# Low-rank products of RWKV-7 as split float32r products, shared scratch, and a changed order of the first receptance, in a fused decoder block on one core

## The chip, the cores and the metric

The kernel runs on one core of one Trainium2 chip. The metric is the device time of one execution in microseconds (us), the median of several runs. One execution is also taken by the hardware profiler; its span, from the first to the last instruction, is what the views of the profile divide up. PE is TensorE's matmul side, PEld its weight loads, DVE VectorE, ACT ScalarE, POOL GpSimd, SP the engine that issues the weight loads from memory.

## The reference, cut to what matters

The whole is one decoder layer for 512 tokens of width 1024: a norm, a combined projection, an attention mixer (NSA), an RWKV-7 mixer, a merge, an output projection, and a convolutional MLP. The change lies in the vectors that the RWKV-7 mixer prepares before its recurrence:

```python
def rwkv7_mixer(p_in, mu, w0, w2, a0, a2, g2, k_k, k_a, r_k, ln_g, ln_b):
    shifted = jnp.pad(p_in, ((0, 0), (1, 0), (0, 0)))[:, :-1]
    xl = p_in + (shifted - p_in) * mu
    r, k, v, xw, xa, xg = jnp.split(xl, RWKV_SPLITS, axis=-1)
    w = -jax.nn.softplus(-(w0 + jnp.tanh(xw) @ w2)) - 0.5
    decay = jnp.exp(-jnp.exp(w))
    a = jax.nn.sigmoid(a0 + xa @ a2)
    g = jax.nn.sigmoid(xg) @ g2
    ...
    kk = k * k_k
    kk = kk / jnp.maximum(jnp.sqrt(jnp.sum(kk * kk, axis=-1, keepdims=True)), 1e-12)
    k = k * (1.0 + (a - 1.0) * k_a)
    ...
```

The two low-rank products are tanh(xw) @ w2 (decay) and xa @ a2 (learning rate): 512 tokens, depth 64 each, 512 channels out.

## The kernel before, in words

**Layout.** Activations stand with channels on the 128 partitions and the 512 tokens along the free dimension, so a "dense" product of one weight tile (1024 deep, 128 channels) fills one PSUM bank of 128x512. The normalised input is kept as two float32r parts, hh and hl; each weight tile is loaded by SP into `raw` (three buffers), copied by ACT to its float32r high part `whi` and subtracted by DVE (some by POOL) to the low part `wlo` (two buffers each). A dense product (`dense_fm`, recorded at L120) is 24 passes of 512 columns: eight of whi by hh and eight of whi by hl in turn, then eight of wlo by hh. `wnext` issues the next load and the next split whenever a tile is taken.

**Who sets the order.** Engines run their own instructions in a fixed order and wait on semaphores. In parts marked `manual_schedule` that order is as written. Elsewhere, and so in all of the part around the change, a planner sets it when the program is built: it follows estimated times, and among instructions that it takes to be ready it prefers the one written earlier. Tiles with one tag share one buffer; a new tile of a tag waits until all users of the old one are done.

**The RWKV preparation (about 20 to 124 us).** p0 is the dense product that yields xw (rows 0 to 63) and xa (rows 64 to 127). `shift_mix` mixes each token with the one before it (ACT at L123, DVE at L135); tanh is taken of xw's half. `sg` comes from a second dense product. wa holds w2 on partitions 0 to 63 and a2 on 64 to 127; POOL issues its two loads (L435, L436), and g2's (L437). POOL then issues the loads of later parameters into prb and cr. Then, for each of four head pairs p:

- `front(p)`: the dense key product pk, then the two low-rank products: zw (`wa[0:64]` by `xw[0:64]`, bank ps_a) and za (`wa[64:128]` by `xw[64:128]`, bank ps_b), both in float32. From zw come cl (tanh), its running sum cum within chunks of 64 tokens, and the exponentials ep and pi; from za comes aa.
- `norms(p)`: kk, the squared scaled keys (ACT), then the sum over each head as a product with the block matrix `ones` in float32 (ps_a<-kk,kc), then rn by DVE's maximum and ACT's Ln and Exp.
- `receptance(p)`, `values_of(p)`: dense products r and v, mixed into rx and vx.
- `vectors(p)` (DVE): AR from rx and ep, kk times rn, bh (keys by pi), tv (rx by r_k by kx); tv's sum over heads is another product with `ones` (ps_a<-tv,kc), which gives BO.
- `values_tok(p)` (L540) and `gram(p)` (L571 and on): transposes of vx and bh, and products of bh and AR, masked into AB.

The order written is `front(0)`, `norms(0)`, `receptance(0)`, `values_of(0)`, `late_params()` (transposes of prb and cr, L478 to L483), and then the loop over p, with `front(p + 1)` and `norms(p + 1)` ahead of `vectors(p)`. The weight tiles come in the order key, receptance, value of each pair.

**After it.** DVE inverts 64 small triangular matrices (transposes at L623, 31 steps, transposes at L728 and L733) beside dense products; PE reads the inverse in `below` (32x32 products). Then come the recurrence, with g2 used in its group norm, attention, the merge and the MLP.

Of the kernel before, what the change touches and what calls it, by code (L numbers as in the profile page):

```python
# [10 lines left out]
F32 = mybir.dt.float32  # L11
F32R = mybir.dt.float32r
I32 = mybir.dt.int32
AF = mybir.ActivationFunctionType
ALU = mybir.AluOpType
# [4 lines left out]
S = 512  # L20
# [27 lines left out]
NROWS = _n  # L48
NR0 = ROWS["ffn_norm_g"][0]
# [31 lines left out]
def hybrid_block(ctx: ExitStack, tc: tile.TileContext, A: dict, out: bass.AP):  # L81
    nc = tc.nc
# [16 lines left out]
    def pool(name, side="left"):  # L99
        cm = tc.tile_pool(name=name, bufs=1, side=side)  # L100
        return cm, cm.__enter__()

    def close(cm):
        cm.__exit__(None, None, None)
# [8 lines left out]
    def pa():  # L113
        return bank("a", 2)

    def pb():
        return bank("b", 2)

    def mm(o, l, r, start, stop):
        te.matmul(o, lhsT=l, rhs=r, start=start, stop=stop)  # L120

    def act(o, i, f=AF.Copy, **kw):
        sc.activation(o, i, f, **kw)  # L123

    def tt(o, a, b, op):
        v.tensor_tensor(o, a, b, op=op)  # L126

    def ts(o, a, s1, s2, op0=ALU.mult, op1=ALU.add):
        if s2 is None:
            v.tensor_scalar(o, a, s1, None, op0=op0)  # L130
        else:
            v.tensor_scalar(o, a, s1, s2, op0=op0, op1=op1)

    def stt(o, a, s, b, op0=ALU.mult, op1=ALU.add):
        v.scalar_tensor_tensor(o, a, s, b, op0=op0, op1=op1)  # L135
# [20 lines left out]
    for name in ("rwkv_mu", "rwkv_w0", "rwkv_a0", "rwkv_k_k", "rwkv_k_a", "rwkv_r_k", "rwkv_ln_g", "rwkv_ln_b"):  # L156
        r0, n = ROWS[name]
        src = A[name]
        if name == "rwkv_r_k":
            src = src.rearrange("l h d -> l (h d)")  # L160
# [7 lines left out]
    def col(name, i=0):  # L168
        r0, n = ROWS[name]
        return prm[:, r0 + i:r0 + i + 1]  # L170
# [158 lines left out]
    with tc.manual_schedule(engines={getattr(mybir.EngineType, e) for e in ("PE", "Activation", "DVE", "Pool")}):  # L329
# [18 lines left out]
        hi = wp.tile([128, KT, 128], F32R, name="whi", tag="whi", bufs=2)  # L348
        lo = wp.tile([128, KT, 128], F32R, name="wlo", tag="wlo", bufs=2)
# [43 lines left out]
    def run(g):  # L393
        while True:
            try:
                next(g)
            except StopIteration as e:
                return e.value

    def dense_fm_g(xh, xl, kt=KT):  # L400
        hi, lo = wnext(kt, 128)
        p = mmb()
        for k in range(kt):
            mm(p, hi[:, k], xh[:, k], k == 0, False)
            mm(p, hi[:, k], xl[:, k], False, False)
            if 4 * k == 3 * kt - 4:
                yield
        for k in range(kt):
            mm(p, lo[:, k], xh[:, k], False, k == kt - 1)
        return p  # L410

    def dense_fm(xh, xl, kt=KT):
        return run(dense_fm_g(xh, xl, kt))


    gp_cm, gp = pool("tb", "right")
# [3 lines left out]
    tp_cm, tp = pool("rtmp")  # L420
# [6 lines left out]
    BO = gp.tile([128, 4, S], F32, name="BO", tag="BO")  # L427
    PC = rp.tile([128, NH2, NCH], F32, name="PC")
    sg = gp.tile([128, S], F32, name="sg", tag="sg")
    g2 = gp.tile([128, 512], F32, name="g2", tag="g2")  # L430
    scanm = tp.tile([128, NCH, C], F32, name="scanm")
    v.memset(scanm, 1.0)
    v.memset(scanm[:, :, 0:1], 0.0)
    wa = tp.tile([128, 512], F32, name="wa")
    nc.gpsimd.dma_start(wa[0:64], A["rwkv_w2"][0])  # L435
    nc.gpsimd.dma_start(wa[64:128], A["rwkv_a2"][0])  # L436
    nc.gpsimd.dma_start(g2, A["rwkv_g2"][0])  # L437

    def shift_mix(p, m, dst):
        mu = col("rwkv_mu", m)  # L440
        act(dst, p, AF.Copy, scale=omm[:, m:m + 1])
        stt(dst[:, 1:], p[:, :-1], mu, dst[:, 1:])

    def t2(name, bufs=1):
        return tp.tile([128, S], F32, name=name, tag=name, bufs=bufs)

    xw = t2("xw")
    shift_mix(p0, 12, xw)
    act(xw[0:64], xw[0:64], AF.Tanh)
    shift_mix(dense_fm(hh, hl), 13, sg)  # L450

    act(sg, sg, AF.Tanh, scale=0.5)
    ts(sg, sg, 0.25, 0.25)


    prb = tp.tile([NROWS - NR0, 128], F32, name="prb")
    for name, (r0, n) in ROWS.items():
        if r0 >= NR0:
            r0 -= NR0
            src = A[name]  # L460
            if name.startswith("cmp_pe"):
                src = src.rearrange("l a d -> l (a d)")
# [2 lines left out]
                nc.gpsimd.dma_start(prb[r0:r0 + 1, 64:128], src)  # L465
            else:
                nc.gpsimd.dma_start(prb[r0:r0 + n], src[0].rearrange("(r p) -> r p", p=128))
    cr = tp.tile([88, 2, 128], F32, name="cr")
    nc.gpsimd.dma_start(cr[0:44, 0], A["conv_w"][0, 0].rearrange("(r p) -> r p", p=128))
    nc.gpsimd.dma_start(cr[44:88, 0], A["conv_w"][0, 1].rearrange("(r p) -> r p", p=128))  # L470
    nc.gpsimd.dma_start(cr[0:44, 1], A["conv_w"][0, 2].rearrange("(r p) -> r p", p=128))
# [1 line left out]
    def chunks(ap):  # L473
        return ap.rearrange("p (c t) -> p c t", t=C)
# [15 lines left out]
    def front(p):  # L490
        cs = slice(128 * p, 128 * p + 128)
        kx = t2("kx", 2)
        pk = dense_fm(hh, hl)
        zw, za = pa(), pb()
        mm(zw, wa[0:64, cs], xw[0:64], True, True)
        mm(za, wa[64:128, cs], xw[64:128], True, True)
        shift_mix(pk, 4 + p, kx)
        cl = t2("cl")
        act(cl, zw, AF.Tanh, scale=0.5, bias=w0h[:, p:p + 1])
        aa = t2("aa", 2)  # L500
        act(aa, za, AF.Tanh, scale=0.5, bias=a0h[:, p:p + 1])
        ts(cl, cl, -0.5 * DECAY, -0.5 * DECAY)
        cum = t2("cum")
        v.tensor_tensor_scan(out=cum, data0=scanm.rearrange("p c t -> p (c t)"), data1=cl, initial=0.0,
                             op0=ALU.mult, op1=ALU.add)
        ep = tp.tile([128, NCH, C + 1], F32, name="ep", tag="ep", bufs=2)
        v.memset(ep[:, :, 0:1], 1.0)
        act(ep[:, :, 1:], chunks(cum), AF.Exp)
        pi = t2("pi", 2)
        act(pi, cum, AF.Exp, scale=-1.0)  # L510
        v.tensor_copy(PC[:, p, :, None], ep[:, :, C:C + 1])
        L[p] = dict(kx=kx, aa=aa, ep=ep, pi=pi)

    def norms(p):
        kx = L[p]["kx"]
        kk = t2("kk", 2)
        act(kk, kx, AF.Square, scale=col("rwkv_k_k", p))
        ss = pa()
        mm(ss, ones, kk, True, True)
        rn = t2("rn", 2)  # L520
        ts(rn, ss, 1e-24, None, op0=ALU.max)
        act(rn, rn, AF.Ln)
        act(rn, rn, AF.Exp, scale=-0.5)
        L[p].update(kk=kk, rn=rn)

    def receptance(p):
        rx = t2("rx", 2)
        shift_mix(dense_fm(hh, hl), p, rx)
        L[p]["rx"] = rx

    def values_of(p):
        vx = t2("vx")
        shift_mix(dense_fm(hh, hl), 8 + p, vx)
        L[p]["vx"] = vx
# [50 lines left out]


    front(0)
    norms(0)
    receptance(0)
    values_of(0)  # L590
    late_params()
    for p in range(NH2):
        if p + 1 < NH2:
            front(p + 1)
            norms(p + 1)
        values_tok(p)
        vectors(p)
        if p + 1 < NH2:
            receptance(p + 1)
        gram(p)  # L600
        if p + 1 < NH2:
            values_of(p + 1)
        if p + 2 == NH2:
            kcp = dense_fm(hh, hl)
    dbg("AR", AR)
    dbg("BO", BO)
    close(tp_cm)

    m2_cm, m2 = pool("mix2")
    sg_cm, sgp = pool("sig")  # L610
    spare = sgp.tile([128, 2, 1024], F32R, name="spare", tag="sg0")
    sg1 = sgp.tile([128, 4, S], F32, name="sg1", tag="sg1")
    tp_cm, tp = pool("rinv")
# [163 lines left out]
    tp_cm, tp = pool("rseq")  # L777
# [455 lines left out]
    for m in range(KT):  # L1233
        cs = slice(128 * m, 128 * m + 128)
# [50 lines left out]
    with tc.manual_schedule(engines=KTS):  # L1285
# [16 lines left out]
        for pair in range(2):  # L1302
            cs = slice(256 * pair, 256 * pair + 256)
# [37 lines left out]
    for hf in range(2):  # L1341
        bo = dense_tok(512, aT[:, 0], aT[:, 1], NF)
        for t in range(NT):
            n = 256 if hf and t == NT - 1 else 512
            for c0 in range(0, 512, n):
                cs = slice(512 * hf + c0, 512 * hf + c0 + n)
# [30 lines left out]
```

## Time and profile before

| what | us |
|---|---|
| median of 3 runs | 847.76 (847.65 to 847.85) |
| the profiled execution | 847.76 |
| its span | 846.0 |
| PE busy in the span | 831.9 |
| DVE busy | 514.7 |
| ACT busy | 405.7 |
| POOL busy | 52.5 |

Rows of the timeline read: start, duration, engine, line and operation, out<-in, shape, count, and in brackets the idle time of the engine before it with what ended it. Matmuls are pipelined, so their recorded durations overlap, and the distance between starts is the time that one takes from PE. Rows of stages read: stretch, its length, then busy time (and count) of PE, PEld, DVE, ACT and POOL, the granted PE clock, the share of the DMA engines and GB/s. Rows of waits read: engine, line, what it waited for, total us, times, longest.

### The profile page before, as it was taken

How to read it: one execution, taken by the hardware profiler on the slowest of the kernel's cores; microseconds unless marked ns; L12 is line 12 of the kernel's file. 1: busy time of each engine (PE TensorE's matmuls, PEld its weight loads, DVE VectorE, ACT ScalarE, POOL GpSimd, SP SyncE). 2: the span in 40 equal slices, each digit the busy share in tenths (PEclk: the TensorE clock that was granted, in tenths of full speed). 3: DMA queues.
4: the chain of work that ended last, by engine and by line, in shares of the span. 5: the costliest groups of instructions: out<-in, count | busy, mean ns of one | idle time of the engine just before them, and what ended most of it. 6: DMA issues, size and time to landing. Idle time of an engine off the chain costs nothing.

```text
span 846.0 us, 12844 instructions
## 1 busy us (share of the span) xinstructions
PE 831.9 (98%) x5097; PEld 676.2 (80%) x5097; DVE 514.7 (61%) x998; ACT 405.7 (48%) x784; POOL 52.5 (6%) x69
## 2 busy tenths in 40 slices
PE   7999999999999999999999999999999999999998
PEld 6777778897777886777788888888888888888886
DVE  5477779963555678888675566666666666322222
ACT  6766645443545677767344454444444444221210
POOL 6200020140000110111000000000000000000000
PEclk9999999999999999999999999999999999999999
DMA  7432222335551320010167023333333332333421
GB/s 231 112 86 62 75 75 76 92 108 151 132 119 50 83 69 13 15 36 26 52 215 221 0 77 98 100 100 100 100 100 95 90 91 98 100 100 112 136 75 50
DMA packets 109104, 78.73 MB, mean 93 GB/s; under 512 B 3869, under 2 KB 97748, under 8 KB 109044
## 3 DMA queue, kind: packets, MB, share of 16 engines
q1 hardware_dynamic: 106512, 73.51, 29.8%
q0 software_dynamic: 1472, 1.86, 1.0%
q10 hardware_dynamic: 1060, 2.55, 1.0%
q8 instruction: 40, 0.66, 0.3%
q14 instruction: 20, 0.16, 0.1%
HBM read 74.56 MB, written 2.29 MB: 91 GB/s over the span
## 4 chain that ended last, share of the span: by engine, by line
PE 52%; DVE 0%; ACT 0%; DVEq 0%; issue 0%
PE ps_mm L120 52%; DVE hl L135 0%; PE ps_a L120 0%; PE ps_b L1181 0%; PE ps_a L200 0%; PE ps_mm L1181 0%; ACT hh L123 0%; PE ps_b L200 0%; DVE x L126 0%; DVEq L1373 0%; PE ps_a L1133 0%
## 5 line engine op out<-in xcount | busy, mean ns | idle before, releaser
L294 DVE TENSOR_TENSOR wlo<-raw,whi 128x1024 fp32r<-128x1024 f32 (+1 forms) x111 | 131.6, 1185 | 189.4 <-PE ps_mm L120 166.8
L120 PE MATMUL ps_mm<-hh,whi 128*128 128x512 f32 (+1 forms) x624 | 243.3, 392 | 0.4 <-ACT hh L123 0.3
L120 PE MATMUL ps_mm<-hl,whi 128*128 128x512 f32 (+1 forms) x624 | 240.9, 388 | 0.3 <-DVE hl L135 0.2
L123 ACT ACTIVATE whi<-raw 128x1024 fp32r<-128x1024 f32 (+3 forms) x124 | 123.4, 996 | 170.3 <-PE ps_mm L120 142.4
L120 PE MATMUL ps_mm<-hh,wlo 128*128 128x512 f32 (+1 forms) x624 | 151.8, 385 | 0.0
L120 PEld LDWEIGHTS ps_mm<-hh,whi 128*128 128x128 f32 x624 | 117.3, 188 | 27.3 <-issue 1.3
L120 PEld LDWEIGHTS ps_mm<-hl,whi 128*128 128x128 f32 x624 | 117.4, 188 | 24.1 <-DVE hl L135 1.0
L120 PEld LDWEIGHTS ps_mm<-hh,wlo 128*128 128x128 f32 x624 | 115.2, 188 | 23.3
L120 PE MATMUL ps_mm<-whi,aT 128*128 128x512 f32 x352 | 84.5, 390 | 0.0
L120 PEld LDWEIGHTS ps_mm<-whi,aT 128*128 128x128 f32 x352 | 65.9, 188 | 14.3 <-issue 0.4
L135 DVE SCALAR_TENSOR_TENSOR cgv<-ps_mm,cw,cgv 128x511 f32<-128x511 f32 (+1 forms) x88 | 65.4, 746 | 1.5
L123 ACT ACTIVATE cgv<-ps_mm,cw 128x512 f32<-128x512 f32 x44 | 34.3, 781 | 22.8 <-PE ps_mm L120 22.8
L120 PE MATMUL ps_mm<-wlo,aT 128*128 128x512 f32 x176 | 44.3, 390 | 0.0
L123 ACT ACTIVATE P<-P,nm 128x512 f32<-128x512 f32 (+3 forms) x64 | 35.4, 554 | 14.9 <-DVE nm L1155 14.9
L123 ACT ACTIVATE aT<-cgv 128x512 fp32r<-128x512 f32 x22 | 13.9, 631 | 56.8 <-DVE cgv L126 56.8
L120 PEld LDWEIGHTS ps_mm<-wlo,aT 128*128 128x128 f32 x176 | 33.1, 188 | 6.9
L123 ACT ACTIVATE cgv<-cgv 128x512 f32<-128x512 f32 x22 | 13.9, 632 | 43.9 <-DVE cgv L135 43.8
L294 POOL TENSOR_TENSOR wlo<-raw,whi 128x512 fp32r<-128x512 f32 (+3 forms) x13 | 20.4, 1573 | 203.6 <-PE ps_mm L120 147.9
L1155 DVE CUSTOM_DVE_ANT_0 P<-ps_a,AB 128x512 f32<-128x512 f32 (+3 forms) x64 | 29.4, 484 | 4.2 <-PE ps_a L120 3.7
L126 DVE TENSOR_TENSOR x<-x,ps_mm 128x512 f32<-128x512 f32 (+1 forms) x17 | 11.1, 656 | 23.9 <-PE ps_mm L120 22.7
L126 DVE TENSOR_TENSOR aT<-cgv,aT 128x512 fp32r<-128x512 f32 x22 | 15.2, 693 | 14.7 <-ACT aT L123 14.7
L120 PE MATMUL ps_a<-KH,qst 128*128 128x512 f32 (+3 forms) x64 | 21.3, 349 | 1.5 <-DVE nm L1155 0.9
(356 smaller groups left out, 1205.5 us busy)
## 6 DMA issues: line engine op xcount, KB each, us to landing
raw<-in_w_up_dram SPq DMA_DIRECT2D x44, 512.0 KB, 3.8
raw<-in_w_in_dram SPq DMA_DIRECT2D x38, 512.0 KB, 3.9
raw<-in_w_down_dram SPq DMA_DIRECT2D x22, 512.0 KB, 3.6
raw<-in_w_out_dram SPq DMA_DIRECT2D x8, 512.0 KB, 3.7
xt<-in_x_dram SPq DMA_DIRECT2D x4, 512.0 KB, 5.7
raw<-in_cmp_w_k_dram SPq DMA_DIRECT2D x4, 512.0 KB, 4.0
raw<-in_cmp_w_v_dram SPq DMA_DIRECT2D x4, 512.0 KB, 4.4
raw<-in_w_proj_b_dram SPq DMA_DIRECT2D x8, 256.0 KB, 2.7
```

The source lines that it names most:

```text
L120: te.matmul(o, lhsT=l, rhs=r, start=start, stop=stop)
L123: sc.activation(o, i, f, **kw)
L126: v.tensor_tensor(o, a, b, op=op)
L135: v.scalar_tensor_tensor(o, a, s, b, op0=op0, op1=op1)
L294: eng.tensor_tensor(lo, raw, hi.bitcast(F32), op=ALU.subtract)
L1155: v.tensor_tensor_reduce(out=P[:, i], in0=sp[:, N * (i - i0):N * (i - i0) + N], in1=BT[:, h, 384 - 128 * qt:512], scale=-1.0, scalar=-NEG, ...
```

## The change

Four things change.

1. wa and the mixed xw are each split once into a float32r high part (ACT copy) and low part (DVE subtraction): `wap` and `xwp`. Each of zw and za becomes three float32r products (high by high, high by low, low by high) instead of one float32 product.
2. Scratch is shared: xw takes the buffer of tag tv, wa that of vx, wa's high part that of g2, cum is written over cl, and prb and cr become parts of one tile `rows` in the buffer of bh.
3. g2 is allocated and loaded after the preparation instead of before it.
4. `receptance(0)` is written ahead of `norms(0)`.

```diff
-    g2 = gp.tile([128, 512], F32, name="g2", tag="g2")
     scanm = tp.tile([128, NCH, C], F32, name="scanm")
...
-    wa = tp.tile([128, 512], F32, name="wa")
+    xwp = tp.tile([128, 2, S], F32R, name="xwp")
+    wap = [gp.tile([128, S], F32R, name="wa_hi", tag="g2"), tp.tile([128, S], F32R, name="wa_lo")]
+
+    def parts(hi, lo, src):
+        act(hi, src)
+        tt(lo, src, hi.bitcast(F32), ALU.subtract)
+
+    wa = tp.tile([128, 512], F32, name="wa", tag="vx")
     nc.gpsimd.dma_start(wa[0:64], A["rwkv_w2"][0])
     nc.gpsimd.dma_start(wa[64:128], A["rwkv_a2"][0])
-    nc.gpsimd.dma_start(g2, A["rwkv_g2"][0])
...
-    xw = t2("xw")
+    xw = t2("tv")
     shift_mix(p0, 12, xw)
     act(xw[0:64], xw[0:64], AF.Tanh)
+    parts(xwp[:, 0], xwp[:, 1], xw)
+    parts(*wap, wa)
     shift_mix(dense_fm(hh, hl), 13, sg)
...
-    prb = tp.tile([NROWS - NR0, 128], F32, name="prb")
+    rows = tp.tile([128, 3, 128], F32, name="rows", tag="bh")
+    prb, cr = rows[0:NROWS - NR0, 2], rows[0:88, 0:2]
...
-    cr = tp.tile([88, 2, 128], F32, name="cr")
...
-        mm(zw, wa[0:64, cs], xw[0:64], True, True)
-        mm(za, wa[64:128, cs], xw[64:128], True, True)
+        for i, (a, b) in enumerate(((0, 0), (0, 1), (1, 0))):
+            mm(zw, wap[a][0:64, cs], xwp[0:64, b], i == 0, i == 2)
+            mm(za, wap[a][64:128, cs], xwp[64:128, b], i == 0, i == 2)
...
-        cum = t2("cum")
+        cum = cl
...
     front(0)
+    receptance(0)
     norms(0)
-    receptance(0)
     values_of(0)
...
+    g2 = gp.tile([128, 512], F32, name="g2", tag="g2")
+    nc.gpsimd.dma_start(g2, A["rwkv_g2"][0])
     m2_cm, m2 = pool("mix2")
```

## The prediction

> **What bounds the kernel now.** I read the engines' busy time first, then busy time by stage around the change, then what PE waited for between 14 and 180 us, and last the end of the chain of waits.
>
> ```profile
> PE 831.9 (98%) x5097; PEld 676.2 (80%) x5097; DVE 514.7 (61%) x998; ACT 405.7 (48%) x784; POOL 52.5 (6%) x69
> ```
> ```profile
> 31.30:45.00 13.70, 13.56 (x57) 9.70 (x56) 8.81 (x14) 10.23 (x14) 0.00 (x0) 1.00 0.29 77
> 45.00:60.00 15.00, 15.00 (x73) 10.76 (x74) 10.95 (x19) 10.05 (x16) 0.00 (x0) 1.00 0.28 72
> ```
> ```profile
> PE ps_b L540 <- DVE vx L135: 0.2, 1, 0.2
> PE ps_mm L120 <- DVE AB L126: 0.2, 1, 0.2
> ```
> ```profile
> 489.58 352.89 PE ps_mm L120 x1569
> ```
>
> In the stage rows the first sum is PE's: 15.00 of 15.00 us in the stage with the second front, 13.56 of 13.70 in the one with the first. DVE and ACT stay at 11 us of 15 or below, DMA at 0.29 or below. The waits listed between 14 and 180 us come to 0.4 us, and the chain ends in 352.89 us of unbroken dense products. So a microsecond less on PE before 105 us should come off the end, and ACT, DVE or DMA work beside PE is free until it makes PE wait.
>
> **The low-rank products.** Before, each front has a block of two float32 products, 64 rows deep, one on partitions 0 to 63 and one on 64 to 127. Each product is recorded as two passes, and the passes stand in pairs:
>
> ```profile
> 31.31 0.69 PE L120 MATMUL ps_a<-xw,wa 64*128 64x512 f32 x1
> 31.32 0.69 PE L120 MATMUL ps_b<-xw,wa 64*128 64x512 f32 x1
> 31.84 0.59 PE L120 MATMUL ps_a<-xw,wa 64*128 64x512 f32 x1
> 31.85 0.59 PE L120 MATMUL ps_b<-xw,wa 64*128 64x512 f32 x1
> 32.37 0.50 PE L120 MATMUL ps_mm<-hh,whi 128*128 128x512 f32 x1
> 32.70 0.39 PE L120 MATMUL ps_mm<-hl,whi 128*128 128x512 f32 x1
> 32.93 0.40 PE L120 MATMUL ps_mm<-hh,whi 128*128 128x512 f32 x1
> ```
> ```profile
> L120 PE MATMUL ps_a<-xw,wa x8: 589/642/694, 31.3 to 96.3; 64*128 64x512 f32 x8
> ```
> ```profile
> 54.43 1.02 PE L120 MATMUL ps_a<-kk,kc 128*128 128x512 f32 x2
> 55.29 1.02 PE L120 MATMUL ps_a<-tv,kc 128*128 128x512 f32 x2
> ```
>
> I take starts, because the durations overlap. The block runs from 31.31 to 32.37, 1.06 us; eight passes on each bank make four such blocks. A float32 product of 512 columns between others takes two passes in 55.29 - 54.43 = 0.86 us, 0.43 a pass. So 1.06 is 0.86 of streaming and 0.20 of edges. The loads of weights show the edges:
>
> ```profile
> 31.31 0.18 PEld L120 LDWEIGHTS ps_a<-xw,wa 64*128 64x128 f32 x1 [0.35 <-issue]
> 31.32 0.18 PEld L120 LDWEIGHTS ps_b<-xw,wa 64*128 64x128 f32 x1
> 31.42 0.19 PEld L120 LDWEIGHTS ps_a<-xw,wa 64*128 64x128 f32 x1
> 31.42 0.19 PEld L120 LDWEIGHTS ps_b<-xw,wa 64*128 64x128 f32 x1
> 32.37 0.19 PEld L120 LDWEIGHTS ps_mm<-hh,whi 128*128 128x128 f32 x1 [0.76 <-ACT kx L123]
> ```
>
> The first load and the first pass start together, so some 0.11 us (31.31 to 31.42) is paid openly; the other 0.09 stands ahead of 32.37, where the next dense load begins only as its product does. Both belong to going from 128 rows to 64 and back, and I keep them.
>
> After, each block has three passes on each half (high by high, high by low, low by high), in float32r. A dense float32r pass of 512 columns takes 32.93 - 32.70 = 0.23 us. No float32r product 64 rows deep stands in this trace. From below: three pair slots without edges, 3 x 0.23 = 0.69, a gain of 0.37 a block. From above: six passes one after another, each with its load of 0.11 paid openly, 6 x 0.34 + 0.09 = 2.13, a loss of 1.07. I take pairs side by side with edges, 3 x 0.23 + 0.20 = 0.89, as the nearest row (the float32 pairs in the same places, 0.01 apart) has it: **0.17 gained a block, 0.68 in four**.
>
> By the Trainium skill ("TensorEngine Tiling (Array Packing)", Key Properties), a change of tiling mode drains TensorE. The trace agrees so far as 0.20 us of edges goes; by that rule the edges stay whatever the type, which gives 0.68, and without it up to 1.48.
>
> **The first receptance.** Before, the sum over heads of the first front (`ones` by kk) was put into the middle of the receptance product:
>
> ```profile
> 33.86 0.40 PE L120 MATMUL ps_mm<-hh,whi 128*128 128x512 f32 x1
> 34.40 1.13 PE L120 MATMUL ps_a<-kk,kc 128*128 128x512 f32 x2
> 34.96 0.79 PE L120 MATMUL ps_mm<-hl,whi 128*128 128x512 f32 x1
> 35.59 0.40 PE L120 MATMUL ps_mm<-hh,whi 128*128 128x512 f32 x1
> ```
> ```profile
> 34.40 0.30 PEld L120 LDWEIGHTS ps_a<-kk,kc 128*128 128x128 f32 x2 [0.58 <-ACT kk L123]
> ```
>
> From 33.86 to 35.59 are 1.73 us; two dense passes take 0.46 of it, the sum over heads 0.86, so 0.41 is wait and an uncovered load, and the load names ACT's kk. With receptance ahead in program order, its 24 passes are ready and go first; the sum follows at about 37.7, some 3 us after kk is there. **0.41 gained**; at worst nothing, or a loss if what depends on the sum comes late. What is late next is rn, then DVE's kk and the rest of that head pair:
>
> ```profile
> 40.34 0.63 ACT L123 ACTIVATE rn<-rn 128x512 f32<-128x512 f32 x1
> ```
> ```profile
> 42.25 0.74 DVE L135 SCALAR_TENSOR_TENSOR kk<-kx,prm,rn 128x512 f32<-128x512 f32 x1
> 50.12 0.74 DVE L135 SCALAR_TENSOR_TENSOR tv<-rx,prm,kx 128x512 f32<-128x512 f32 x1
> ```
>
> The sum ends 3.3 us later than before (35.36 to about 38.6), but rn's last step was itself held behind a weight split on ACT; I estimate kk at 43 to 44.5 instead of 42.25. In return rx and its product with ep, two DVE instructions behind rn before, go ahead of it. tv (50.12) ends at 50.86 and its product stands at 55.29, 4.4 us of cover; only a delay beyond that costs PE, one for one.
>
> **The splits.** They add two ACT copies and two DVE subtractions of 128x512 once. Rows of the same shape and types:
>
> ```profile
> L123 ACT ACTIVATE aT<-cgv 128x512 fp32r<-128x512 f32 x22 | 13.9, 631 | 56.8 <-DVE cgv L126 56.8
> ...
> L126 DVE TENSOR_TENSOR aT<-cgv,aT 128x512 fp32r<-128x512 f32 x22 | 15.2, 693 | 14.7 <-ACT aT L123 14.7
> ```
> ```profile
> wa<-in_rwkv_a_dram POOLq DMA_DIRECT2D x1, 128.0 KB, 4.9
> ```
> ```profile
> 20.47 0.52 POOL L436 DMA_DIRECT2D wa<-in_rwkv_a_dram  x1
> ```
> ```profile
> 24.21 1.06 ACT L123 ACTIVATE whi<-raw 128x1024 fp32r<-128x1024 f32 x1 [0.44 <-PE ps_mm L120]
> ```
> The copy takes 0.63 us and the subtraction 0.69. wa lands at 20.47 + 4.9 = 25.4; a copy and a subtraction bring its parts to 26.7, some 28 behind other work; the block starts at 31.31. This is the one added wait: wa's copy may stand in ACT's queue ahead of the split of whi (24.21), which then ends at about 27 instead of 25.3, and DVE's subtraction for it, and sg's mixing, come behind. PE needs that whi at 32.37, so 4 us cover it: nothing. If wa were 4 us later, PE would wait one for one.
>
> **Shared scratch.** xw stands in tv's place, wa in vx's, cum in cl's, the parameter rows in bh's, wa's high part in g2's. xw and wa are read for the last time before 30 us, vx and tv written after 44. bh's first write now waits for the transposes of the parameter rows:
>
> ```profile
> 45.11 0.24 PE L483 MATMUL ps_a<-kc,cr 88*128 88x88 f32 x1
> ```
> ```profile
> 44.96 0.69 DVE L135 SCALAR_TENSOR_TENSOR bh<-kk,pi 128x512 f32<-128x512 f32 x1
> ```
> ```profile
> 59.68 0.27 PE L571 MATMUL ps_b<-kc,bh 64*128 64x64 f32 x1
> ```
> The last transpose ends at 45.35, so the write at 44.96 can be held 0.4 us; PE reads bh at 59.68: nothing. g2's load leaves the front of POOL's queue and must wait for the last block, whose last pass starts at 96.3:
>
> ```profile
> 118.42 2.35 POOL L294 TENSOR_TENSOR wlo<-raw,whi 128x1024 fp32r<-128x1024 f32 x1 [90.62 <-PE ps_mm L120]
> ```
> POOL sits idle for 90.62 us up to 118.42, so an issue as long as wa's 0.52 fits in, and g2 is first read in the recurrence, behind the inverse. Nothing; 0.5 if it meets the split at 118.42. That the early load is gone I cost at nothing too: the stages that gain from it are ahead of wa's issue, and there PE is paced by x and its normalisation; the other end is some tenths gained.
>
> **The sum.** 4 x 0.17 + 0.41 = 1.09 us. The profiled execution took 847.76 us (span 846.0, 1.76 around it), which is also the median of the three runs: **846.7**. Does the gain last? The widest DVE stage is the inverse:
>
> ```profile
> 163.02 4.51 DVE L728 STREAM_TRANSPOSE sg<-inv 32x1024 f32<-32x1024 f32 x2
> ```
> ```profile
> 168.72 0.21 PE L120 MATMUL ps_a<-sg,AB 32*32 32x32 f32 x1
> ```
> It ends at 167.53, 1.19 us before PE reads it. That chain starts behind PE's last gram product, so it should move forward with PE; even if it stood still, 1.19 covers 1.09.
>
> **Rivals.** (a) *Loads not covered.* Three slots of 0.23 + 0.11, and 0.09: 1.11 a block, +0.05; in four +0.2, less 0.41: 847.6. Against it: the second pair of loads starts at 31.42, while the first pair still streams to 31.84 on the same rows. This is what the Trainium skill ("TensorE: Matmul & The Clock Gate", Part 3, What overlaps and what doesn't) would make of it: a load overlaps running products only on other row groups; the load at 31.42 speaks against that here. (b) *Slower: float32r halves run one after the other.* Place: the block; price 6 x 0.23 + 0.20 = 1.58, +0.52, in four +2.1, less 0.41: 849.4, and 851.6 with open loads (4 x 1.07 - 0.41). It decides from a slot of (1.06 + 0.10 - 0.20) / 3 = 0.32 us on. For it: no such pair is in the trace; against: float32 pairs start 0.01 apart. (c) *A new wait.* The planner orders by its own estimates, and PE holds one order; kk's wait of 0.3 came so. One or two such waits, or a late tv, eat the gain: 847.5 to 848.5. (d) *No edges, or a wait at 118.5 or 124 falls away too:* 4 x 0.37 + 0.41 = 1.89: 845.9. (e) *Receptance isn't moved by the planner:* 847.1, within the forecast.
>
> **Chances.** Forecast with (e), 846.3 to 847.2: 0.64. (a) 0.09, (b) 0.10, (c) 0.10, (d) 0.07. The range 845.8 to 848.3 leaves out (b) and the upper end of (c). A measurement of this kernel tells from no change about 0.2%, 1.7 us: faster means below 846.07, slower above 849.46. Faster has (d) and the forecast's lower tail, 0.12; slower has the upper half of (b) and a large (c), 0.10; within 0.2%, 0.78.
>
> **What would show it.** Right: in each of four blocks six float32r passes, zw and za starting together, slots 0.23 apart, the next product 0.89 after the first; the sum over heads after 24 unbroken receptance passes; PE's first 32x32 product 1.1 us earlier, at 167.6. Wrong: slots of 0.32 or more, or PE waits that name ACT wa, DVE tv or DVE bh.

## The result

| what | before | after |
|---|---|---|
| median of 6 executions, us | 847.86 (847.65 to 848.04) | 852.54 (850.93 to 853.21) |
| the profiled execution, us | 847.76 | 850.93 |
| its span, us | 846.0 | 849.1 |

The ratio of after to before is 1.0051, with a 95% interval of 1.0038 to 1.0064: slower by 0.5%, and outside the range of the prediction. Two of the six executions of after had a granted TensorE clock of 1.000 and took 850.93 and 851.03 us; four had 0.996 to 0.998 and took 852.44 to 853.21. The profiled one is of the first kind, so the profile can explain 3.1 us of the span, and some 1.5 us of the median are not in it.

The profile after, first the page's busy times, then PE's waits between 14 and 180 us (engine, line, what it waited for, total, times, longest):

```profile
PE 831.8 (98%) x5105; PEld 676.6 (80%) x5105; DVE 516.8 (61%) x1000; ACT 407.3 (48%) x786; POOL 52.5 (6%) x69
```
```profile
PE ps_b L548 <- DVE vx L135: 1.9, 3, 1.0
PE ps_a L120 <- DVE tv L135: 1.5, 1, 1.5
PE ps_a L120 <- ACT kk L123: 0.3, 1, 0.3
```

PE's busy time has not changed, but it now waits 3.7 us in this window, where it had 0.4 in this view before and 0.3 ahead of the first sum over heads (starts 33.86 and 34.40, less a pass of 0.23). That is 3.0 more; the shorter products give 0.7 back, the front starts 0.2 later (31.53 for 31.31), and the remaining 0.6 lies in no wait that is listed. The timeline of PE shows that the two things that were forecast did happen:

```profile
31.53 0.49 PE L120 MATMUL ps_a<-xwp,wa_hi 64*128 64x512 f32 x1
31.53 0.49 PE L120 MATMUL ps_b<-xwp,wa_hi 64*128 64x512 f32 x1
31.87 0.39 PE L120 MATMUL ps_a<-xwp,wa_hi 64*128 64x512 f32 x1
...
32.09 0.39 PE L120 MATMUL ps_a<-xwp,wa_lo 64*128 64x512 f32 x1
...
32.41 0.50 PE L120 MATMUL ps_mm<-hh,whi 128*128 128x512 f32 x1
...
38.01 1.02 PE L120 MATMUL ps_a<-kk,kc 128*128 128x512 f32 x2
```

and of the weight loads for the second and third pair:

```profile
31.64 0.19 PEld L120 LDWEIGHTS ps_a<-xwp,wa_hi 64*128 64x128 f32 x1
...
31.87 0.18 PEld L120 LDWEIGHTS ps_a<-xwp,wa_lo 64*128 64x128 f32 x1
```

The block runs from 31.53 to 32.41, 0.88 us; the next pairs follow 0.34 and 0.22 after the one ahead. The receptance runs through from 32.41 and the sum over heads follows at 38.01. What was lost lies behind this, in three places.

**rn is late.** The timeline of DVE and ACT around the first pair's reciprocal norm, before (the exponential at 40.34 and kk at 42.25 stand in the prediction) and after:

```profile
35.73 0.69 DVE L130 TENSOR_SCALAR rn<-ps_a 128x512 f32<-128x512 f32 x1
...
37.45 0.63 ACT L123 ACTIVATE rn<-rn 128x512 f32<-128x512 f32 x1
37.99 1.04 ACT L123 ACTIVATE whi<-raw 128x1024 fp32r<-128x1024 f32 x1
```
```profile
40.48 0.68 DVE L130 TENSOR_SCALAR rn<-ps_a 128x512 f32<-128x512 f32 x1
...
41.20 0.63 ACT L123 ACTIVATE rn<-rn 128x512 f32<-128x512 f32 x1 [1.00 <-DVE rn L130]
42.72 1.06 ACT L123 ACTIVATE whi<-raw 128x1024 fp32r<-128x1024 f32 x1 [0.89 <-PE ps_mm L120]
43.80 1.28 ACT L123 ACT_TABLE_LOAD   x1
45.09 0.63 ACT L123 ACTIVATE rn<-rn 128x512 f32<-128x512 f32 x1
...
45.76 0.75 DVE L135 SCALAR_TENSOR_TENSOR kk<-kx,prm,rn 128x512 f32<-128x512 f32 x1 [3.99 <-ACT rn L123]
```

rn has three steps: a maximum on DVE (40.48), then the logarithm (41.20) and the exponential (45.09) on ACT. The maximum comes 4.75 us later than before: the sum over heads starts 3.6 us later, and DVE now has a weight split and rx ahead of the maximum. Between logarithm and exponential stand a weight split and a table load, as they did before, but now the split waits 0.89 us for PE to free its buffer, and the exponential too is 4.75 us late. Before, kk had stood 1.3 us behind the exponential's end, and that slack is used up: DVE idles 3.99 us and starts kk at 45.76 instead of 42.25, 3.5 us late.

**The lag stays.** The first scaling of rx on DVE in pairs two to four, before and after:

```profile
62.37 0.75 DVE L135 SCALAR_TENSOR_TENSOR rx<-ps_mm,prm,rx 128x511 f32<-128x511 f32 x1 [1.30 <-ACT rx L123]
84.85 0.75 DVE L135 SCALAR_TENSOR_TENSOR rx<-ps_mm,prm,rx 128x511 f32<-128x511 f32 x1 [1.31 <-ACT rx L123]
107.32 0.75 DVE L135 SCALAR_TENSOR_TENSOR rx<-ps_mm,prm,rx 128x511 f32<-128x511 f32 x1 [1.31 <-ACT rx L123]
```
```profile
64.22 0.75 DVE L135 SCALAR_TENSOR_TENSOR rx<-ps_mm,prm,rx 128x511 f32<-128x511 f32 x1 [1.43 <-ACT rx L123]
86.83 0.75 DVE L135 SCALAR_TENSOR_TENSOR rx<-ps_mm,prm,rx 128x511 f32<-128x511 f32 x1 [1.44 <-ACT rx L123]
109.43 0.75 DVE L135 SCALAR_TENSOR_TENSOR rx<-ps_mm,prm,rx 128x511 f32<-128x511 f32 x1 [1.43 <-ACT rx L123]
```

After, rx is 1.85, 1.98 and 2.11 us late. The distance from pair to pair is 22.48 and 22.47 us before, 22.61 and 22.60 after, although PE has less to do.

**tv is held.** The last pair after, on DVE, POOL and PE:

```profile
119.31 0.74 DVE L135 SCALAR_TENSOR_TENSOR vx<-ps_mm,prm,vx 128x511 f32<-128x511 f32 x1
119.97 2.18 DVE L135 SCALAR_TENSOR_TENSOR tv<-rx,prm,kx 128x512 f32<-128x512 f32 x1
...
119.20 2.39 POOL L294 TENSOR_TENSOR wlo<-raw,whi 128x1024 fp32r<-128x1024 f32 x1 [21.23 <-PE ps_mm L120]
...
120.11 0.66 PE L548 MATMUL ps_b<-kc,vx 128*128 128x128 f32 x4 [1.05 <-DVE vx L135]
122.29 1.10 PE L120 MATMUL ps_a<-tv,kc 128*128 128x512 f32 x2 [1.53 <-DVE tv L135]
```

tv takes 2.18 us instead of 0.75: it ends at 122.15, 0.56 after POOL's split of the query weights ends (121.59). Before, it ran here:

```profile
115.93 0.75 DVE L135 SCALAR_TENSOR_TENSOR tv<-rx,prm,kx 128x512 f32<-128x512 f32 x1
```
It stood ahead of a weight split and of vx on DVE, and was done before POOL began at 118.42. After, the planner has put both ahead of it in pairs two to four.

### The profile page after: what moved, and what is told of

Its sections match the earlier page's. It is cut to its first block, busy times and chain, and to the rows that moved or that the text cites. A ratio compares the mean times of both kernels' runs of the same rounds, so it can differ in the third digit from the quotient of the medians.

```text
span 849.1 us, 12867 instructions
## 1 busy us (share of the span) xinstructions
PE 831.8 (98%) x5105; PEld 676.6 (80%) x5105; DVE 516.8 (61%) x1000; ACT 407.3 (48%) x786; POOL 52.5 (6%) x69
## 4 chain that ended last, share of the span: by engine, by line
PE 52%; DVE 0%; ACT 0%; DVEq 0%; issue 0%
PE ps_mm L120 51%; DVE hl L135 0%; PE ps_a L120 0%; PE ps_b L1191 0%; PE ps_a L200 0%; PE ps_mm L1191 0%; ACT hh L123 0%; PE ps_b L200 0%; DVE x L126 0%; DVEq L1383 0%; PE ps_a L1143 0%
```

## The experiments

All times are medians; e1 to e4 ran against 847.78 us for the kernel before, e5 to e8 against 847.87, e9 to e12 against 847.74. My theory from this profile had three parts: **M**, the moved receptance makes rn late and the lag stays; **O**, the shorter products make the planner put tv behind; **P**, what makes tv late there is POOL's split. The rival to each was that one of the others does it all.

**e1: without the move.**
```diff
     front(0)
-    receptance(0)
     norms(0)
+    receptance(0)
```


> Undoes only the reordering of the first receptance; the split products and the shared scratch stay. Theory M (the move is what costs: the first rn comes 3.5 us late because its Exp stands behind a weight split on ACT that waits for PE, and the lag of DVE then never heals): DVE's first kk no later than 42.5 us, PE waits of at most 0.8 us in all between 14 and 180 us, and the time is the forecast without the 0.41: 847.1 (846.6 to 847.7). Theory O (the shorter products make the planner put the weight split and vx ahead of tv on DVE in the later rounds, and that is what PE waits for): the waits on vx and tv at about 120 us stay, 2 to 3 us in all, and the time is 849.5 to 851.5.

850.37 us (849.24 to 852.12), ratio 1.0032 [1.0023, 1.0041]; PE's waits:
```profile
PE ps_a L120 <- DVE tv L135: 1.8, 1, 1.8
PE ps_b L548 <- DVE vx L135: 0.8, 1, 0.8
```
```profile
118.04 2.40 DVE L135 SCALAR_TENSOR_TENSOR tv<-rx,prm,kx 128x512 f32<-128x512 f32 x1
```
kk starts at 42.38 again, so the late rn is gone, but tv lasts 2.40 us. M alone fails, O holds.

**e2: the move alone**, in the kernel before.
```diff
     front(0)
+    receptance(0)
     norms(0)
-    receptance(0)
```


> The kernel before with the first receptance moved and nothing else: float32 products, separate scratch. Theory M: DVE's first kk at 45 us or later, lag in every round, PE waits of 2 us or more, 850 to 851.5. Theory O: the later rounds keep the order of before (tv ahead of the split and vx), no waits of PE on tv, 847.4 (847.0 to 848.2).

849.54 us, ratio 1.0020 [1.0011, 1.0029]. The waits and DVE's kk:
```profile
PE ps_b L540 <- DVE vx L135: 1.2, 2, 0.9
PE ps_a L120 <- ACT kk L123: 0.8, 1, 0.8
```
```profile
45.82 0.75 DVE L135 SCALAR_TENSOR_TENSOR kk<-kx,prm,rn 128x512 f32<-128x512 f32 x1 [4.40 <-ACT rn L123]
```
The move costs 1.8 us without any of the rest, which is 0.5 us less than M's lowest. rx is 1.80, 1.80 and 1.82 us behind before in pairs two to four, about as much as the time is longer. tv isn't held here. So O alone fails too: there are two causes.

**e3: sharing and splits alone.** Order of before, and one float32 product of the high parts in place of three; the low parts are left out of the sum.
```diff
+        mm(zw, wap[0].bitcast(F32)[0:64, cs], xwp[0:64, 0].bitcast(F32), True, True)
+        mm(za, wap[0].bitcast(F32)[64:128, cs], xwp[64:128, 0].bitcast(F32), True, True)
```


> The shared scratch and the two splits stay, the order of the first receptance is that of before, and the low-rank products are one float32 product each, of the high parts alone (the low parts are left out of the sum). Theory M and theory O: no effect of the sharing itself, 847.9 (847.5 to 848.4), the blocks 1.06 us again. A third theory S (a tile waits for the buffer it now shares): 849 or more, with waits of DVE on bh, vx or tv.

848.11 us, ratio 1.0003 [0.9995, 1.0012], waits of 0.5 us for 0.4, tv ahead of vx. Sharing, splits and the late load of g2 cost nothing that can be seen. e1 differs from this kernel in the products alone, so it is they that turn the order; whether by their shorter time or by their greater number is not shown.

**e4: the whole change, POOL's split of the query weights given to DVE.**
```diff
-        yield from rows(w_in, O_Q, 512, eng=[v, pool_, ("spare", pool_), v])
+        yield from rows(w_in, O_Q, 512, eng=[v, v, ("spare", pool_), v])
```


> The changed kernel, but the second weight tile of the queries is split by DVE behind tv instead of by POOL beside it. tv of the last head pair took 2.18 us instead of 0.74, and it ended 0.6 us after POOL's 2.39 us subtraction. Theory P (an all-SBUF instruction of DVE is held while POOL's subtraction runs): tv takes 0.74 us again, PE's wait on tv falls from 1.5 to 0.1 us, and the time falls by 1.0 to 1.5 us, less up to 0.6 for DVE's extra 1.22: 849.4 to 850.2 in executions at full clock. If POOL has nothing to do with it: tv stays at 2.2 us and the time at 850.9 or above.

849.66 us, ratio 1.0022 [1.0013, 1.0031]. The longest waits, and tv in the last pair:
```profile
PE ps_b L548 <- DVE vx L135: 2.0, 3, 1.1
```
```profile
119.59 0.74 DVE L135 SCALAR_TENSOR_TENSOR tv<-rx,prm,kx 128x512 f32<-128x512 f32 x1
```
tv is 0.74 long in the same place of the order, and PE doesn't wait for it: P holds. That is 2.9 us less than after, and 1.3 less than the two executions of after with a granted clock of 1.000.

**e5 and e6: tv first, without and with the move.**
```diff
-        stt(tv, rx, col("rwkv_r_k", p), kx, ALU.mult, ALU.mult)
+        with tc.high_priority():
+            stt(tv, rx, col("rwkv_r_k", p), kx, ALU.mult, ALU.mult)
```


> The change without its move, and VectorE's product tv given a higher priority in the planner, so that it stands ahead of the wlo split and of vx in each round, as it does in the kernel before; nothing else moves. Theory of the planner's order: the TensorE wait of 1.8 us on tv at 120 us goes, a wait on vx of 0.8 to 1.4 us stays; the time is 847.3 to 848.3 us, and the granted clock is 0.999 or more in every execution. Rival (VectorE is held by GpSimd's split wherever tv stands, since that split fills the window): tv still lasts over 1.5 us in the last round and the time is 849.5 us or more.

> The whole change, with tv given the same higher priority. Theory of two causes: the wait on tv goes, but the lag from the late reciprocal norm stays (VectorE's kk of the first pair still starts after 45 us, the waits on vx still sum to 2.5 us or more), so the time is 849.0 to 850.0 us, 1.0 to 1.7 above the run before it in this list. Rival (the order alone decides, the move costs nothing): 847.3 to 848.3, as without the move.

e5: 848.09 us, ratio 1.0004 [0.9995, 1.0013]. e6: 849.83, 1.0023 [1.0014, 1.0033]. The waits of e5, and what POOL's split meets instead of tv:
```profile
PE ps_b L548 <- DVE vx L135: 0.9, 1, 0.9
PE ps_b L580 <- DVE bh L135: 0.8, 1, 0.8
```
```profile
118.06 2.31 DVE L135 SCALAR_TENSOR_TENSOR bh<-kx,pi 128x512 f32<-128x512 f32 x1
...
117.47 2.35 POOL L294 TENSOR_TENSOR wlo<-raw,whi 128x1024 fp32r<-128x1024 f32 x1 [20.91 <-PE ps_mm L120]
```
Both times fit the theory of two causes, with 1.7 us between them for the move. But the hold was only handed on: the priority put tv ahead of bh too, bh now stands where tv had stood and takes 2.31 us instead of 0.69, and PE waits 0.8 for it. In e6 the waits on vx sum to 1.4, not 2.5 as expected; 1.0 for kk and 0.7 for bh stand in their place.

**e7: without the move, POOL's split on DVE** (the edits of e1 and e4).

> The change without its move, with the second split of the query weights on VectorE instead of GpSimd; the planner's order of tv is left as it is. Theory that GpSimd's split holds tv: tv lasts 0.7 to 0.8 us in the last round and TensorE does not wait for it beyond 0.3; the time is 847.2 to 848.3 us. Rival (the lateness of tv comes from its place alone, not from being held): the wait on tv stays over 1 us and the time is 849.3 or more.

847.88 us, ratio 1.0000 [0.9991, 1.0009], and one wait is left:
```profile
PE ps_b L548 <- DVE vx L135: 0.8, 1, 0.8
```
With both causes gone the kernel is as fast as before, not 0.7 us faster. PE does gain: its blocks start at 50.60, 72.89 and 95.18, 22.29 apart instead of 22.47. Then it waits 0.76 us for vx at 118.29. DVE's rx comes at 62.42, 85.02 and 107.62, still 22.60 apart: DVE does not follow PE.

That made a new theory, **the loop**. In before, the rows of the timeline go round from one pair's rx (84.85, shown above) to the next:
```profile
98.17 1.22 DVE L504 TENSOR_TENSOR_SCAN cum<-scanm,cl 128x512 f32<-128x512 f32 x1
...
99.42 0.63 ACT L123 ACTIVATE ep<-cum 128x512 f32<-128x512 f32 x1 [0.25 <-DVE cum L504]
...
106.60 0.69 ACT L123 ACTIVATE rx<-ps_mm,omm 128x512 f32<-128x512 f32 x1
```
From 84.85 to the end of cum (99.39) DVE has no gap; from ep (99.42) to rx (106.60) ACT has none: ep, pi, three copies of UV, a table load, the logarithm, a weight split, a table load, the exponential, rx. Then DVE's rx again at 107.32. No row in these stretches shows a wait for PE. So the loop may take 22.47 us by itself, which is PE's own round (50.79 to 73.26 in the rows of zw), and each would hide the other. In e7 it takes 22.60, again without a gap: rx to ep is 14.69 us there (62.42 to 77.11) instead of 14.57. The planner has put AR<-kk,ep directly ahead of kk<-aa,kk, which starts 0.71 us behind it; before, two other products stood between them.

**e8: a late rn in the kernel before.** Six copies of rn onto itself on ACT between logarithm and exponential of the first pair.
```diff
         act(rn, rn, AF.Ln)
+        for i in range(6 if p == 0 else 0):
+            act(rn, rn)
         act(rn, rn, AF.Exp, scale=-0.5)
```


> The kernel before, unmoved and with float32 products, with six copies of rn onto itself on ScalarE between Ln and Exp of the first pair alone: 3 to 3.5 us of extra work ahead of one Exp, once; the result is the same. Theory that a lag does not heal: VectorE's kk starts at 45 to 46.5 us instead of 42.25, VectorE's rx of the next three pairs come 1.0 to 2.5 us late and 22.4 to 22.7 us apart, TensorE waits for vx 0.8 us or more in the third and last rounds; the time is 848.8 to 850.0. Rival (the lag heals within a round, and what is late with the moved receptance is another thing, its place in the order): rx of the third pair is within 0.3 us of the kernel before, and the time is 847.6 to 848.2.

849.47 us, ratio 1.0018 [1.0009, 1.0027]:
```profile
64.04 0.75 DVE L135 SCALAR_TENSOR_TENSOR rx<-ps_mm,prm,rx 128x511 f32<-128x511 f32 x1 [1.44 <-ACT rx L123]
86.51 0.75 DVE L135 SCALAR_TENSOR_TENSOR rx<-ps_mm,prm,rx 128x511 f32<-128x511 f32 x1 [1.43 <-ACT rx L123]
108.99 0.75 DVE L135 SCALAR_TENSOR_TENSOR rx<-ps_mm,prm,rx 128x511 f32<-128x511 f32 x1 [1.43 <-ACT rx L123]
```
kk came later than I meant (48.07), but the test is clear: rx is 1.67, 1.66 and 1.67 us behind before, and the time is 1.60 longer. One delay, put in once, neither heals nor grows in 45 us, and PE pays for it (waits on vx 1.6). What is left of it after the first round does not follow kk alone: kk 5.8 us late leaves 1.67 here, 3.5 late leaves 1.85 in after.

**e9, e10, e11, e12: a shorter loop.** Two of DVE's instructions go to ACT, in a stretch where ACT idles: in e9 without the move, in e10 in the kernel before, in e11 in the whole change; e12 is e9 with the copy of bh alone.
```diff
-        v.tensor_copy(bh[64:128, :, 2, :], bh[64:128, :, 0, :])
-        ts(aa, aa, kah[:, p:p + 1], oma[:, p:p + 1])
+        act(bh[64:128, :, 2, :], bh[64:128, :, 0, :])
+        act(aa, aa, AF.Identity, scale=kah[:, p:p + 1], bias=oma[:, p:p + 1])
```


> The change without its move, and two of VectorE's instructions of each pair given to ScalarE in the stretch where ScalarE idles: the copy of bh (0.43 us) and the scaling of aa (0.54 us). Theory of the loop: VectorE and ScalarE together go round in 22.60 us whatever TensorE does (rx to rx in the last four kernels), TensorE's own round is 22.29 with the shorter products, so 0.97 less on VectorE brings the spacing of rx down to 22.25 to 22.4, the wait on vx under 0.3, and the 0.7 us of the shorter products show at last: 846.8 to 847.5 us. Rival (the order of the products and GpSimd's split decide, no loop): the spacing stays at 22.5 or more, the wait on vx at 0.8, the time at 847.8 to 848.5 as in the run with tv first.

> The kernel before with the same two instructions given to ScalarE and nothing else. Theory of the loop: TensorE's own round is 22.47 us here, as long as the loop, so TensorE stays the bound and only its 0.4 us of waits can go: rx 22.4 to 22.5 apart, 847.3 to 848.0 us. Rival (these two instructions were a bound in themselves, so what helps is not the loop against the shorter products): a gain of 0.6 us or more here as well, 847.2 or less.

> The whole change, the receptance moved, with the same two instructions given to ScalarE. Theory of the loop: the first pair's rn is still 3.5 us late (kk after 45 us), but now the lag shrinks in every round, rx 22.3 apart or less, so the waits on vx sum to under 1.2 us instead of 1.9 with none in the last round, tv is not held, and the time is 846.8 to 848.3 us. Rival (the late rn costs its 1.5 us whatever the loop, as in the run with tv first): 849.2 to 850.2 us.

> The change without its move and with the copy of bh alone (0.43 us) given to ScalarE. Theory of the loop: 22.60 less 0.43 is 22.17, below TensorE's own 22.29, so this does nearly what both do: rx 22.25 to 22.4 apart, 846.9 to 847.7 us. Rival (no loop): as with tv first, 847.8 to 848.5.

| kernel | us | ratio to before | rx to rx, us | waits on vx, us |
|---|---|---|---|---|
| e9, no move | 846.50 | 0.9985 [0.9976, 0.9994] | 21.82, 22.14 | none |
| e12, no move, bh alone | 846.65 | 0.9986 [0.9977, 0.9994] | 22.16, 22.14 | 0.2 |
| e10, before | 847.31 | 0.9995 [0.9986, 1.0004] | 22.48, 22.47 | none |
| e11, whole change | 847.32 | 0.9995 [0.9986, 1.0004] | 21.81, 21.81 | 0.7 |

rx in e9, then in e10, then kk of the first pair and rx in e11:
```profile
62.71 0.75 DVE L135 SCALAR_TENSOR_TENSOR rx<-ps_mm,prm,rx 128x511 f32<-128x511 f32 x1 [1.43 <-ACT rx L123]
84.53 0.75 DVE L135 SCALAR_TENSOR_TENSOR rx<-ps_mm,prm,rx 128x511 f32<-128x511 f32 x1 [1.43 <-ACT rx L123]
106.67 0.75 DVE L135 SCALAR_TENSOR_TENSOR rx<-ps_mm,prm,rx 128x511 f32<-128x511 f32 x1 [1.43 <-ACT rx L123]
```
```profile
85.13 0.75 DVE L135 SCALAR_TENSOR_TENSOR rx<-ps_mm,prm,rx 128x511 f32<-128x511 f32 x1 [1.31 <-ACT rx L123]
107.60 0.75 DVE L135 SCALAR_TENSOR_TENSOR rx<-ps_mm,prm,rx 128x511 f32<-128x511 f32 x1 [1.30 <-ACT rx L123]
```
```profile
45.64 0.75 DVE L135 SCALAR_TENSOR_TENSOR kk<-kx,prm,rn 128x512 f32<-128x512 f32 x1 [4.00 <-ACT rn L123]
...
63.71 0.75 DVE L135 SCALAR_TENSOR_TENSOR rx<-ps_mm,prm,rx 128x511 f32<-128x511 f32 x1 [1.43 <-ACT rx L123]
...
107.33 0.75 DVE L135 SCALAR_TENSOR_TENSOR rx<-ps_mm,prm,rx 128x511 f32<-128x511 f32 x1 [1.43 <-ACT rx L123]
```
The loop holds, and its length can be added up: 22.60 less 0.43 is 22.17, and e12 has 22.16; 22.60 less 0.97 is 21.63, and with the 0.16 us that DVE's kx now waits for ACT's aa it is 21.79, where e9's first distance is 21.82 and e11's are 21.81. I had expected 22.25 or more and, for e9 and e12, 846.8 and 846.9 us at the lowest, so both missed to the good side.

With the loop shortened, the change without its move is worth 847.31 - 846.50 = 0.81 us, where it had been worth nothing in e7. Of PE's work 0.72 less is in the blocks, and some 0.24 in the first pair: without the move the sum over heads now stands one pass further back and waits 0.07 us instead of 0.31. In e10 the loop is as much shorter, but rx stays 22.47 apart: there PE's round is the bound. The interval of e10's ratio takes in no change; of the waits listed, 0.2 on vx has gone and 0.2 on AB has stayed.

In e11 kk is still late at 45.64, but rx catches up, 1.34 late against before at 63.71 and 0.01 at 107.33. In the e9, e11 and e12 kernels DVE has tv ahead of the split and of vx again, so the hold is gone as well; the order is not held fixed in them, and against e5 and e6, where tv is also first, e9 and e11 are 1.6 and 2.5 us faster, of which up to 0.8 is the hold on bh. Against e7, in which nothing is held, e9 is 1.4 faster. e9 and e12 beat both kernels.

## Why the prediction was wrong, point by point

- **The sum.** Of the 5.8 us between the forecast of 846.7 and the 852.54 measured, 1.1 is the gain that does not show, 1.8 the cost of the move (e2), and 2.9 the held tv (after against e4), of which 1.3 at a granted clock of 1.000. The prediction's sum had the first as a gain and the other two at nothing: a late kk and a late tv stood in it only as conditions and in rival (c).
- **The products: right.** 0.88 a block for 0.89, pairs side by side with edges; 0.18 saved in each of four. The rule of the Trainium skill cited for rival (a) ("TensorE: Matmul & The Clock Gate", Part 3, What overlaps and what doesn't) does not hold here: the load for the third pair starts at 31.87 with the second pair, which streams on the same rows, and the third pair follows only 0.22 us behind it, at 32.09.
- **Receptance first: mis-sized and of the wrong sign.** PE's 0.41 came: the sum follows 24 unbroken passes, and e2 goes from the first block to the second in 19.06 us instead of 19.48. After takes 18.89, but e1 has 19.04 without the move, since the planner already lets the sum wait less there; so beside the shorter products the move gives PE 0.15. What failed is the step that allowed kk 43 to 44.5 and gave tv "4.4 us of cover; only a delay beyond that costs PE". kk came at 45.76, because DVE took a weight split and rx ahead of rn's maximum and the weight split between rn's steps on ACT, which had not waited before, waited for PE. And tv was the wrong thing to look at: kk's lateness goes round the loop into the next pairs' rx and vx. Alone it costs 1.8 us (e2).
- **"A microsecond less on PE before 105 us should come off the end", and other work "is free until it makes PE wait": the step under both that failed.** It was read from PE's busy time and from waits of 0.4 us. That shows that PE was hardly kept waiting, not that it was the only bound. The loop was as long as PE's round, 22.47 us, so a saving on PE alone is given back at a later vx (e7, 0.76 us at 118.29), and a delay on DVE stays. The rows were there: the three rx before, and two engines without a gap between them.
- **The free edits: right.** Splits, sharing, g2's load: nothing that can be seen (e3, 0.3 us with an interval that takes in no change).
- **Rival (c)** named the mechanism, the planner's other order and a late tv, but at one or two waits that eat the gain. It did not see that tv, moved by two instructions, comes under POOL's split and grows by 1.4 us; that costs 2.3 to 2.9 us in medians (e1 against e5 and e7; after against e4 and e6), and 1.1 to 1.7 in the executions of e1 and after at 0.999 or more.
- **Rivals (a), (b), (d), (e)** did not occur.
- PE's first 32x32 product, forecast at 167.6, stands at 172.00 after, at 167.39 in e9.

## What to carry over

A bound engine without waits can have a second bound beside it: follow one tile of the loop (here rx) from round to round, and see whether the other engines come round without a gap in the same time; if they do, less work on the first engine shows only when they are shortened too, and here 0.43 us less a round there was worth more than the edit itself. A delay of an instruction in such a loop isn't covered by the slack of its own reader; it returns in every round until the loop has slack to make it up, as in e11. And where a planner orders by its estimates, changing a few instructions changes the order elsewhere: compare each engine's order before the times.

## What the runs showed of the hardware

A DVE instruction with two inputs in SBUF was held while a POOL instruction of that kind ran: tv 2.18 us in after and 2.40 in e1, bh 2.31 in e5 and 2.18 in e6, each 0.69 to 0.75 without POOL. vx, with one input in PSUM, took its 0.74 beside the same split. The Trainium skill ("SBUF — State Buffer", Who interferes with whom) says that a VectorE instruction with two SBUF inputs contends with a GpSimd instruction that reads SBUF, that the shared pair of ports is an exclusive lock, and that the order of issue decides who blocks. The runs agree: each held instruction began after POOL's and ended 0.5 to 0.6 us after it.

The granted clock fell below 0.999 only in the two kernels in which PE waits 1.5 us or more for the held tv: in four of six executions of after, and in six of ten of e1 (850.3 to 852.1 us at 0.996 to 0.998, against 849.24 to 849.76 at 0.999). In the other eleven experiments and in the runs of before that stood beside them it was 0.999 or more throughout, e4 and e6 with single waits of 1.1 us included. That the long wait brings the lower clock is argued from this, not shown: no profile fell into such an execution, so where the clock is lower stays open.
